# A hybrid attention and gating block in split fp32 on one core: first weights of two seven-product stages ahead of the bank reads, operand space opened to the plain stages, later splits for the next stage

## The chip, the cores and the metric

One NeuronCore of a Trainium2 chip runs the whole program; the host only lays the arrays out in the blocks that are loaded. The metric is the device time of one execution in microseconds, lower is better. The kernel before takes 2866.29 us (median of 3 runs, 2864.26 to 2869.96).

## The reference, cut to what matters

One decoder block on 512 tokens of width 2048, all in float32:

```
a = rms_norm(x);  z = a @ w_in          # q_lat 512, kv_lat 512, k_pe 64, u 1024, v 1024, gate logits 2 x 2048
y_attn = mla(q_lat, kv_lat, k_pe) @ w_o_attn          # 16 heads, causal, rotary part of 64
y_sgu  = (gelu(u) * (tril(w_s) v' + b_s)) @ w_o_sgu   # v' = rms_norm(gelu(v)), chunks of 128, 8 groups
h = x + (sigmoid(g0) * y_attn + sigmoid(g1) * y_sgu) @ w_out
f = rms_norm(h)
h = h + (silu(f @ w_gate) * (f @ w_up)) @ w_down      # hidden width 5632
return rms_norm(h)
```

## The kernel before, in words

**Split operands.** A float32 operand is kept as two float32r pieces, a rounded `hi` and the rest `lo`; ACT makes `hi` with a cast and DVE makes `lo` with a subtraction (`split` L134, `chunk` L150 to L157, `form_w` L367 to L372). Each product is three matmuls (`mm3` L168: lo by hi, hi by hi, hi by lo).

**Plain stages.** `gemm_fm` (L172) and `gemm_tm` (L185) take one weight block of 512 KB at a time. `chunk` loads it on the SP queue into a raw tile, makes `hi` and `lo`, and 24 matmuls with 512 columns follow. Plain stages are: the latents and the v half of the gating input (L277 to L352, 16 chunks of `w_v`), the attention pairs (L745 to L766), `sgu_out` (L732, 8 calls of two chunks), the attention output (L774 to L789), `w_out` (L820 to L847) and `w_down` (L900 to L909, 80 chunks).

**Seven-product stages.** `run` (L463) multiplies blocks with seven products in place of eight, each of 24 matmuls with 256 columns: once for u and both gates (L533, 20 blocks), once for the FFN's gate and up weights (L889, 44 blocks). `Unit.weights(i)` forms the i-th of seven weight combinations on DVE and splits it; `multiply` issues the matmuls, `read` empties the three banks. These are pinned to program order among themselves on each engine; everything else is placed by the scheduler of the framework. The moving operands are eight `forms` of 14 units each, made by `forms_x` (L320): four subtractions, one cast on ACT and one subtraction on DVE. Six of the eight forms are made while the plain stage in front still runs. `run` starts with weights 0 to 2, multiplies them by the six forms, calls `rest()` (L488; `x_rest` L528 or `f_rest` L850) for the last two forms, then loads `unit(1)` and goes on. At the end of its last block it calls the functions in `ends`, by the number of the product just issued.

**Reads of the stage in front.** For the first seven-product stage the eight banks of the v products are read before `run` is called (L357 to L362): per bank a Gelu, a Square that sums into `vacc` and a store to `vvd`. For the second, the loop at L820 to L847 adds x to each bank, squares, scales by `r0` and stores to `hd`, all before `run`. `rv` (L579 to L581) is the norm factor from `vacc`; `spatial` (L583) uses it in pairs 0 and 1 of the attention loop (L754).

**Space.** `Arena` hands out pieces of two big SBUF tiles, `ar` (144 units, operands) and `af` (52 units, float32), in program order. Its rule (L65 to L68) is the cost by which a free place is chosen:

```
cost = (i,) if low else (n < self.large and i < self.keep, n < 8 and self.pack and None not in block,
                         max(span), -i)
```

So a small piece goes to a place at or above `keep` if any is free there, however lately that place was given back (`max(span)` comes third), and only then to the place given back longest ago. `ar.keep` is NX = 112 through the whole kernel, `ar` has 144 units, and a chunk needs two pieces of 4. A piece that was used shortly before makes the new writer wait for the matmuls that still read it.

**Loads.** `load` and `store` go through the POOL queue, weights through SP. `latents(g)` (L264) loads four tiles, transposes on PE and splits; it is called after products 2 and 4 of the last block (L533). `hidden(k0, n)` (L886) loads and splits tiles of the FFN's hidden values, after products 2 and 4 of the last block (L889). The residual tiles `h` are loaded from `hd` right after (L892 to L894).

Of the kernel before, what the change touches and what calls it, by code (L numbers as in the profile page):

```python
# [12 lines left out]
AF = mybir.ActivationFunctionType  # L13
# [75 lines left out]
def tile_block(ctx: ExitStack, tc, a):  # L89
# [9 lines left out]
    def T():  # L99
        return af.get(2)  # L100
# [58 lines left out]
    def load(src):  # L159
        t = T()  # L160
        nc.gpsimd.dma_start(t, src)
        return t
# [101 lines left out]
    def latents(g):  # L264

        zs, rows = [load(latd[g, tb]) for tb in range(NB)], []
        for k in range(4):
            ps = PS()
            for tb in range(NB):
                nc.tensor.transpose(out=ps[:, tb * P:(tb + 1) * P], in_=zs[tb][:, k * P:(k + 1) * P], identity=ident)  # L270
            v = (V_Q, V_KV)[g] + k
            rows.append(split(ps, vec[:, v:v + 1]))
        drop(zs)
        return rows
# [82 lines left out]
    for tb in range(NB):  # L357
        for g in range(2):
            t = T()
            nc.scalar.activation(t, banks[g][tb], AF.Gelu_apprx_tanh, scale=rx[:, tb:tb + 1])  # L360
            nc.scalar.activation(junk, t, AF.Square, accum_out=vacc[:, tb * 2 + g:tb * 2 + g + 1])
            store(vvd[g, tb], t)  # L362
# [100 lines left out]
    def run(jobs, fx, rest, ends, lead=3):  # L463
# [12 lines left out]
        for g in range(last + 7 + lead + 1):  # L476
# [7 lines left out]
            if g == lead - 1:  # L484
                early = len(fx)
                for i in range(lead):
                    units[0].multiply(i, ready[i], fx, range(early))
                rest()  # L488
                unit(1)
# [9 lines left out]
        af.keep, af.pack = 0, False  # L499
# [28 lines left out]
    def x_rest():  # L528
        x_forms(6)
        x_forms(7)  # L530

    latT = []
    run(x_jobs(), fx, x_rest, {2: lambda: latT.append(latents(0)), 4: lambda: latT.append(latents(1))})  # L533
# [45 lines left out]
    vs2 = small(NB, "vs2")  # L579
    nc.vector.tensor_reduce(out=vs2, in_=vacc.rearrange("p (n k) -> p n k", k=2), axis=AX.X, op=ALU.add)  # L580
    rv = rsqrt(vs2, SGUW, NB, "rv")  # L581
# [163 lines left out]
    for pr in range(NP):  # L745
# [8 lines left out]
        if pr < 2:  # L754
            spatial(pr)
# [18 lines left out]

    oT = [move(load(ogd[k]), low=True) for k in range(KD)]
# [46 lines left out]
    for c in range(4):  # L822
# [13 lines left out]
        hs[c] = []  # L836
        for tb, ps in enumerate(banks):
            tt(ht[tb], ps, ht[tb], ALU.add)
            nc.scalar.activation(junk, ht[tb], AF.Square, accum_out=facc[:, c * NB + tb:c * NB + tb + 1])
            if c == 0 and tb == NB - 1:  # L840
                r0 = rsqrt(facc[:, :NB], D // 4, NB, "r0")
        for tb in range(NB):
            t = T()
            nc.scalar.activation(t, ht[tb], AF.Copy, scale=r0[:, tb:tb + 1])
            hs[c].append(t)
            store(hd[tb, :, c * 512:(c + 1) * 512], ht[tb])
# [4 lines left out]
    def f_rest():  # L851
        scaled(3)
        f_forms(6)
        f_forms(7)
        nc.vector.tensor_reduce(out=fs, in_=facc.rearrange("p (c n) -> p n c", c=4), axis=AX.X, op=ALU.add)
        rf = rsqrt(fs, D, NB, "rf")
        nc.vector.reciprocal(rest, r0)
        tt(rest, rest, rf, ALU.mult)
        row_bcast(rest, rxb)
# [25 lines left out]

    def hidden(k0, n):  # L886
        return [move(load(hidd[k])) for k in range(k0, k0 + n)]

    run(ffn_jobs(), ff, f_rest, {2: lambda: hid.extend(hidden(0, 4)), 4: lambda: hid.extend(hidden(4, 4))})  # L889


    for tb in range(NB):  # L892
        for c in range(4):
            h[tb][c] = load(hd[tb, :, c * 512:(c + 1) * 512])  # L894
# [5 lines left out]
    for k0 in range(0, 40, 8):  # L900
        nxt, n = [], 2 if k0 < 32 else 1
        for c in range(4):
            nxt += hidden(k0 + 8 + c * n, n)
# [127 lines left out]
```

## Time and profile before

| | |
|---|---|
| median of 3 runs | 2866.29 us (2864.26 to 2869.96) |
| the profiled execution | 2865.04 us; its span 2863.3 us |
| mean granted TensorE clock | 0.979 of full speed |
| busy, of the span | PE 2725.3 us (95%), DVE 1739.3 us (61%), ACT 1094.0 us (38%), POOL 197.3 us (7%) |
| read from HBM, written | 315.07 MB, 45.35 MB, 126 GB/s over the span |

The profile shows one execution. Matmuls overlap, so a PE that counts as busy may still run at half clock or with few matmuls; the number of matmuls in a stretch tells more. "Idle before" of an instruction is the time in which its engine had nothing to do, with the instruction that ended the wait. The 1.7 us between the span and the profiled execution's time lie outside the recorded instructions.

### The profile page before, as it was taken

The numbers are of one execution on the slowest core, as the hardware profiler recorded it, in microseconds if no ns is written. First come the engines' busy times: TensorE is split into PE (matmuls) and PEld (weight loads), VectorE is DVE, ScalarE is ACT, GpSimd is POOL, SyncE is SP. The second block draws the span as 40 slices with busy tenths as digits, with TensorE's granted clock in tenths as the row PEclk, the third lists the DMA queues.
The fourth block names the chain that finished last, engine by engine and source line by source line (L and its number), as shares of the span: only waits on it lengthen the run. The fifth ranks groups of instructions, "written<-read, shape, count | busy, mean of one in ns | idle before, by whom it ended". The sixth has DMA issues, their size and how long they took to land. (4 is left out here: it accounts for less than half of the span.)

```text
span 2863.3 us, 41568 instructions
## 1 busy us (share of the span) xinstructions
PE 2725.3 (95%) x17320; PEld 2479.6 (87%) x17320; DVE 1739.3 (61%) x2200; ACT 1094.0 (38%) x1534; POOL 197.3 (7%) x369
## 2 busy tenths in 40 slices
PE   8989999998999779999889999999999989999998
PEld 6879999987888558888789999999999978787786
DVE  5637777786666233333377877877878763443336
ACT  5334444454555122224344444444344441221224
POOL 1000000011002121000000000000000020000000
PEclk9999999999999889999989999999999989999999
DMA  7423333352324454434223333232333352442333
GB/s 293 157 98 111 140 118 140 118 170 89 103 74 148 132 183 148 129 114 140 88 99 130 115 115 133 104 126 104 133 108 125 114 200 89 146 140 67 103 110 118
DMA packets 103901, 363.13 MB, mean 127 GB/s; under 512 B 14177, under 2 KB 14177, under 8 KB 103713
## 3 DMA queue, kind: packets, MB, share of 16 engines
q1 hardware_dynamic: 72720, 260.60, 26.1%
q0 software_dynamic: 29552, 97.28, 10.1%
q8 instruction: 135, 2.21, 0.3%
q10 hardware_dynamic: 1440, 2.60, 0.3%
q14 instruction: 54, 0.43, 0.0%
HBM read 315.07 MB, written 45.35 MB: 126 GB/s over the span
## 5 line engine op out<-in xcount | busy, mean ns | idle before, releaser
L382 PE MATMUL b<-ar 128*128 128x256 f32 x3584 | 1021.9, 285 | 23.9 <-DVE ar L371 14.6
L384 PE MATMUL b<-ar 128*128 128x256 f32 x3584 | 1020.9, 285 | 3.4 <-DVE ar L119 3.4
L383 PE MATMUL b<-ar 128*128 128x256 f32 x3584 | 1020.3, 285 | 0.0
L169 PE MATMUL b<-ar 128*128 128x512 f32 (+1 forms) x2016 | 780.8, 388 | 95.9 <-DVE ar L155 51.0
L170 PE MATMUL b<-ar 128*128 128x512 f32 (+1 forms) x2016 | 773.8, 384 | 0.0
L171 PE MATMUL b<-ar 128*128 128x512 f32 (+1 forms) x2016 | 762.5, 383 | 0.1
L382 PEld LDWEIGHTS b<-ar 128*128 128x128 f32 x3584 | 694.5, 194 | 26.3 <-DVE ar L371 9.0
L384 PEld LDWEIGHTS b<-ar 128*128 128x128 f32 x3584 | 694.4, 194 | 4.1 <-DVE ar L119 4.1
L371 DVE TENSOR_TENSOR ar<-af,ar 128x1024 fp32r<-128x1024 f32 x448 | 544.3, 1223 | 248.8 <-ACT ar L370 247.4
L383 PEld LDWEIGHTS b<-ar 128*128 128x128 f32 x3584 | 694.5, 194 | 0.0
L370 ACT CAST ar<-af 128x1024 fp32r<-128x1024 f32 x448 | 459.3, 1046 | 481.6 <-DVE af L393 367.8
L169 PEld LDWEIGHTS b<-ar 128*128 128x128 f32 x2016 | 386.0, 191 | 186.7 <-ACT ar L154 48.5
L155 DVE TENSOR_TENSOR ar<-af,ar 128x1024 fp32r<-128x1024 f32 (+1 forms) x224 | 267.7, 1204 | 420.8 <-ACT ar L154 414.1
L154 ACT CAST ar<-af 128x1024 fp32r<-128x1024 f32 (+1 forms) x224 | 229.8, 1035 | 663.5 <-PE b L171 354.0
L171 PEld LDWEIGHTS b<-ar 128*128 128x128 f32 x2016 | 385.6, 191 | 75.8 <-DVE ar L155 2.4
L170 PEld LDWEIGHTS b<-ar 128*128 128x128 f32 x2016 | 386.2, 192 | 70.1
L393 DVE TENSOR_TENSOR af<-af 128x1024 f32<-128x1024 f32 x192 | 234.6, 1222 | 4.2
L390 DVE TENSOR_TENSOR af<-b,af 128x256 f32<-128x256 f32 x320 | 134.6, 421 | 20.3 <-PE b L384 17.4
L897 DVE SCALAR_TENSOR_TENSOR af<-b,rest,af 128x512 f32<-128x512 f32 x96 | 71.6, 749 | 118.1 <-PE b L171 118.1
L138 DVE TENSOR_TENSOR ar<-af,ar 128x512 fp32r<-128x512 f32 x100 | 66.4, 688 | 74.7 <-ACT ar L137 74.7
L396 ACT COPY af<-b 128x256 f32<-128x256 f32 x128 | 47.3, 370 | 166.0 <-PE b L384 131.8
L137 ACT CAST ar<-af 128x512 fp32r<-128x512 f32 x100 | 59.6, 619 | 133.1 <-DMA af<-hidd 46.0
(223 smaller groups left out, 1190.9 us busy)
## 6 DMA issues: line engine op xcount, KB each, us to landing
af<-in_w_gate SPq DMA_DIRECT2D x88, 512.0 KB, 5.3
af<-in_w_up SPq DMA_DIRECT2D x88, 512.0 KB, 5.4
af<-in_w_down SPq DMA_DIRECT2D x88, 512.0 KB, 4.2
af<-in_w_g SPq DMA_DIRECT2D x64, 512.0 KB, 5.3
af<-in_w_oattn SPq DMA_DIRECT2D x32, 512.0 KB, 3.5
af<-in_w_out SPq DMA_DIRECT2D x32, 512.0 KB, 3.5
hidd<-af POOLq DMA_DIRECT2D x44, 256.0 KB, 2.6
af<-hidd POOLq DMA_DIRECT2D x44, 256.0 KB, 3.3
```

The source lines that it names most:

```text
L154: nc.scalar.copy(hi[:, :n], raw[:, :n])
L155: nc.vector.tensor_tensor(out=lo[:, :n], in0=raw[:, :n], in1=hi[:, :n].bitcast(F32), op=ALU.subtract)
L169: nc.tensor.matmul(ps, sl, mh, start=first, stop=False)
L170: nc.tensor.matmul(ps, sh, mh, start=False, stop=False)
L171: nc.tensor.matmul(ps, sh, ml, start=False, stop=last)
L370: pin(nc.scalar.copy(hv, src))
L371: pin(nc.vector.tensor_tensor(out=lv, in0=src, in1=hv.bitcast(F32), op=ALU.subtract))
L382: pin(nc.tensor.matmul(ps, lo[:, ks], xh, start=first and kp == 0, stop=False, skip_group_check=True))
L383: pin(nc.tensor.matmul(ps, hi[:, ks], xh, start=False, stop=False, skip_group_check=True))
L384: pin(nc.tensor.matmul(ps, hi[:, ks], xl, start=False, stop=kp == 7, skip_group_check=True))
L390: pin(nc.vector.tensor_tensor(out=out, in0=in0, in1=in1, op=ALU.add))
L393: pin(nc.vector.tensor_tensor(out=out, in0=in0, in1=in1, op=ALU.subtract))
```

## The change

Four things change.

1. `run` calls `rest` in two parts: weights 0 to 2 of the first block come first, then the first part, then the products with the forms that exist, then the second part. For the first stage the first part is the reads of banks 0 to 3 and form 6, the second the reads of banks 4 to 7 and form 7; for the FFN the first part is the adding of x for the last column block, the second the transposes, forms 6 and 7, the squares, the stores and the norm. The Squares of v leave the reads; `v_stats` loads `vvd` again in pair 0 of the attention and squares there, and `spatial` moves to pairs 1 and 2.
2. `ar.keep` becomes 0 at the end of each `run` and NX again ahead of the attention output.
3. The tiles of the next stage: the loads of `latents` come after products 0 and 2, their transposes and splits after 4 and 5; four hidden tiles are loaded after product 1 and split after 4, the other four after 5.
4. The residual tiles `h` are loaded four at a time inside the first pass of `w_down`.

```diff
@@ latents
-    def latents(g):
-
-        zs, rows = [load(latd[g, tb]) for tb in range(NB)], []
+    def lat_in(g):
+        return [load(latd[g, tb]) for tb in range(NB)]
+
+    def latents(g, zs):
+
+        rows = []
@@ after the v products
-    for tb in range(NB):
-        for g in range(2):
+    def v_out(g):
+        for tb, ps in enumerate(banks[g]):
             t = T()
-            nc.scalar.activation(t, banks[g][tb], AF.Gelu_apprx_tanh, scale=rx[:, tb:tb + 1])
-            nc.scalar.activation(junk, t, AF.Square, accum_out=vacc[:, tb * 2 + g:tb * 2 + g + 1])
+            nc.scalar.activation(t, ps, AF.Gelu_apprx_tanh, scale=rx[:, tb:tb + 1])
             store(vvd[g, tb], t)
@@ run
             if g == lead - 1:
+                rest = rest()
+                next(rest)
                 early = len(fx)
                 for i in range(lead):
                     units[0].multiply(i, ready[i], fx, range(early))
-                rest()
+                for _ in rest:
+                    pass
                 unit(1)
...
-        af.keep, af.pack = 0, False
+        af.keep, af.pack, ar.keep = 0, False, 0
@@ first seven-product stage
     def x_rest():
+        v_out(0)
         x_forms(6)
+        yield
+        v_out(1)
         x_forms(7)
...
-    run(x_jobs(), fx, x_rest, {2: lambda: latT.append(latents(0)), 4: lambda: latT.append(latents(1))})
+    run(x_jobs(), fx, x_rest, {0: lambda: zs.append(lat_in(0)), 2: lambda: zs.append(lat_in(1)),
+                               4: lambda: latT.append(latents(0, zs[0])), 5: lambda: latT.append(latents(1, zs[1]))})
@@ attention
-    vs2 = small(NB, "vs2")
-    nc.vector.tensor_reduce(out=vs2, in_=vacc.rearrange("p (n k) -> p n k", k=2), axis=AX.X, op=ALU.add)
-    rv = rsqrt(vs2, SGUW, NB, "rv")
+    def v_stats():
+        for g in range(2):
+            for tb in range(NB):
+                t = load(vvd[g, tb])
+                nc.scalar.activation(junk, t, AF.Square, accum_out=vacc[:, tb * 2 + g:tb * 2 + g + 1])
+                drop(t)
+        vs2 = small(NB, "vs2")
+        nc.vector.tensor_reduce(out=vs2, in_=vacc.rearrange("p (n k) -> p n k", k=2), axis=AX.X, op=ALU.add)
+        return rsqrt(vs2, SGUW, NB, "rv")
...
-        if pr < 2:
-            spatial(pr)
+        if pr == 0:
+            rv = v_stats()
+        elif pr < 3:
+            spatial(pr - 1)
...
+    ar.keep = NX
     oT = [move(load(ogd[k]), low=True) for k in range(KD)]
@@ w_out, per column block c
+        def add_x(c=c, ht=ht, banks=banks):
+            hs[c] = []
+            for tb, ps in enumerate(banks):
+                tt(ht[tb], ps, ht[tb], ALU.add)
+                if c:
+                    t = T()
+                    nc.scalar.activation(t, ht[tb], AF.Copy, scale=r0[:, tb:tb + 1])
+                    hs[c].append(t)
...
+        elif c < 3:
+            add_x()
+            squares()
+            keep_h()
@@ FFN
     def f_rest():
+        add_x()
+        yield
         scaled(3)
         f_forms(6)
         f_forms(7)
+        squares()
+        keep_h()
...
+    def split_hidden():
+        hid[:4] = [move(t) for t in hid[:4]]
+
+    run(ffn_jobs(), ff, f_rest, {1: lambda: hid.extend(hidden_in(0, 4)), 4: split_hidden,
+                                 5: lambda: hid.extend(hidden(4, 4))})
...
-    for tb in range(NB):
-        for c in range(4):
-            h[tb][c] = load(hd[tb, :, c * 512:(c + 1) * 512])
@@ w_down
         for c in range(4):
+            for tb in range(NB if k0 == 0 else 0):
+                h[tb][c] = load(hd[tb, :, c * 512:(c + 1) * 512])
             nxt += hidden(k0 + 8 + c * n, n)
```

`squares` and `keep_h` are the old Square and store of the loop at L835 to L847, in functions of their own; for column block 0 the order of the old loop stays but for the stores, which come last.

## Rows read from the trace of the kernel before

**Rows 1.** Page, part 1: busy time and instructions of each engine.
```profile
PE 2725.3 (95%) x17320; PEld 2479.6 (87%) x17320; DVE 1739.3 (61%) x2200; ACT 1094.0 (38%) x1534; POOL 197.3 (7%) x369
```

**Rows 2.** Windows: stretch, length, busy us (instructions) of PE, PEld, DVE, ACT, POOL, clock, DMA, GB/s.
```profile
475.00:500.00 25.00, 25.00 (x210) 25.00 (x210) 18.78 (x20) 11.12 (x13) 1.08 (x2) 1.00 0.38 144
...
195.00:230.00 35.00, 20.67 (x104) 19.45 (x104) 24.43 (x35) 16.05 (x23) 2.17 (x4) 0.71 0.16 51
600.00:645.00 45.00, 39.12 (x264) 35.76 (x263) 38.96 (x56) 25.61 (x36) 11.56 (x21) 0.96 0.61 199
690.00:706.00 16.00, 10.48 (x48) 9.39 (x47) 8.58 (x24) 6.72 (x19) 3.84 (x7) 0.79 0.43 140
935.90:1063.00 127.10, 91.29 (x314) 69.37 (x312) 35.63 (x42) 25.24 (x32) 22.04 (x41) 0.85 0.45 139
1428.00:1460.00 32.00, 21.52 (x125) 19.63 (x124) 23.08 (x36) 15.71 (x22) 1.08 (x2) 0.73 0.24 87
2325.00:2350.00 25.00, 12.74 (x88) 12.34 (x86) 11.55 (x18) 8.05 (x14) 9.17 (x18) 0.77 0.62 201
2350.00:2375.00 25.00, 24.76 (x97) 19.84 (x98) 18.80 (x19) 15.78 (x19) 3.69 (x7) 0.89 0.94 347
2423.00:2800.00 377.00, 362.28 (x1568) 291.99 (x1567) 144.53 (x159) 84.81 (x95) 13.97 (x26) 1.00 0.34 110
```

**Rows 3.** Timeline of ACT, attention output stage: start, us, line, operation [idle before <-releaser].
```profile
1149.12 1.05 ACT L154 CAST ar<-af 128x1024 fp32r<-128x1024 f32 x1 [4.39 <-PE b L171]
...
1154.56 1.05 ACT L154 CAST ar<-af 128x1024 fp32r<-128x1024 f32 x1 [0.69 <-PE b L171]
```

**Rows 4.** Timeline of ACT in the calls of `sgu_out`, two chunks in a row.
```profile
936.31 1.04 ACT L154 CAST ar<-af 128x1024 fp32r<-128x1024 f32 x1 [8.48 <-PE b L171]
946.04 1.04 ACT L154 CAST ar<-af 128x1024 fp32r<-128x1024 f32 x1 [8.69 <-PE b L171]
```

**Rows 5.** Waits of PE, 900 to 1066 us: for whom, us in total, times, longest.
```profile
PE b L169 <- DVE ar L155: 38.4, 14, 4.5
```

**Rows 6.** All waits, 2385 to 2860 us: those of PE for chunks.
```profile
PE b L169 <- ACT ar L154: 14.5, 18, 1.4
```

**Rows 7.** Waits of PE, 590 to 930 us (attention).
```profile
PE b L169 <- DVE ar L155: 12.6, 8, 3.8
```

**Rows 8.** Groups by line: the Squares of v; busy us, mean ns, idle before.
```profile
L361 ACT ACTIVATE junk<-af 128x512 f32<-128x512 f32 x8 | 5.0, 626 | 0.1
```

**Rows 9.** DMA issues: tile, queue, count, KB each, median us to landing.
```profile
af<-in_w_ukv SPq DMA_DIRECT2D x16, 512.0 KB, 4.2
...
af<-vvd POOLq DMA_DIRECT2D x8, 256.0 KB, 4.2
```

**Rows 10.** Timeline of ACT in pair 0: the first Exp and its table.
```profile
652.65 1.28 ACT L699 ACT_TABLE_LOAD   x1
653.94 0.40 ACT L699 ACTIVATE af<-af,nm 128x128 f32<-128x128 f32 x1
```

**Rows 11.** Timelines of DVE and PE where the v products end and the first `run` starts.
```profile
198.50 0.16 DVE L580 TENSOR_REDUCE vs<-vacc 128x4 f32<-128x8 f32 x1 [22.45 <-ACT junk L361]
...
218.04 2.02 DVE L119 TENSOR_TENSOR ar<-af,ar 128x1792 fp32r<-128x1792 f32 x1 [1.75 <-ACT ar L330]
...
200.72 0.58 PE L382 MATMUL b<-ar 128*128 128x256 f32 x1 [5.50 <-DVE ar L371]
```

**Rows 12.** Timelines of DVE and PE where `w_out` ends and the FFN's `run` starts.
```profile
1448.06 3.96 DVE L119 TENSOR_TENSOR ar<-af,ar 128x1792 fp32r<-128x1792 f32 x2
...
1432.84 0.55 PE L382 MATMUL b<-ar 128*128 128x256 f32 x1 [4.50 <-DVE ar L371]
```

**Rows 13.** Timelines of ACT and PE where the FFN's `run` ends and `w_down` starts.
```profile
2330.22 1.22 ACT L137 CAST ar<-af 128x512 fp32r<-128x512 f32 x2 [4.13 <-DMA af<-hidd]
...
2334.03 0.58 PE L382 MATMUL b<-ar 128*128 128x256 f32 x1 [4.34 <-DVE af L390]
2350.20 0.80 PE L169 MATMUL b<-ar 128*128 128x512 f32 x1 [8.12 <-ACT ar L154]
```

More of the change, by code (lines that the diff above doesn't have):

```diff
@@ L528, in x_rest @@
     def x_rest():
+        v_out(0)
         x_forms(6)
+        yield
+        v_out(1)
         x_forms(7)
-    latT = []
-    run(x_jobs(), fx, x_rest, {2: lambda: latT.append(latents(0)), 4: lambda: latT.append(latents(1))})
+    latT, zs = [], []
+    run(x_jobs(), fx, x_rest, {0: lambda: zs.append(lat_in(0)), 2: lambda: zs.append(lat_in(1)),
+                               4: lambda: latT.append(latents(0, zs[0])), 5: lambda: latT.append(latents(1, zs[1]))})
     qnT, kvT = latT
@@ L835, in tile_block, with squares, keep_h @@
                 f_forms(order[c, kp])
[L836 to L841, printed above, removed]
-        for tb in range(NB):
[L843 to L846, printed above, removed]
+        def add_x(c=c, ht=ht, banks=banks):
[6 more added lines that the diff above has]
+                    hs[c].append(t)
+        def squares(c=c, ht=ht):
+            for tb in range(NB):
+                nc.scalar.activation(junk, ht[tb], AF.Square, accum_out=facc[:, c * NB + tb:c * NB + tb + 1])
+        def keep_h(c=c, ht=ht):
+            for tb in range(NB):
+                store(hd[tb, :, c * 512:(c + 1) * 512], ht[tb])
+        if c == 0:
+            add_x()
+            squares()
+            r0 = rsqrt(facc[:, :NB], D // 4, NB, "r0")
+            for tb in range(NB):
+                t = T()
+                nc.scalar.activation(t, ht[tb], AF.Copy, scale=r0[:, tb:tb + 1])
+                hs[0].append(t)
+            keep_h()
[3 more added lines that the diff above has]
+            keep_h()
     fs = small(NB, "fs")
@@ L851, in f_rest @@
     def f_rest():
+        add_x()
+        yield
         scaled(3)
@@ L854, in f_rest @@
         f_forms(7)
+        squares()
+        keep_h()
         nc.vector.tensor_reduce(out=fs, in_=facc.rearrange("p (c n) -> p n c", c=4), axis=AX.X, op=ALU.add)
@@ L884, in tile_block, with hidden_in @@
     hid, h = [], [[None] * 4 for _ in range(NB)]
+    def hidden_in(k0, n):
+        return [load(hidd[k]) for k in range(k0, k0 + n)]
     def hidden(k0, n):
-        return [move(load(hidd[k])) for k in range(k0, k0 + n)]
-    run(ffn_jobs(), ff, f_rest, {2: lambda: hid.extend(hidden(0, 4)), 4: lambda: hid.extend(hidden(4, 4))})
-    for tb in range(NB):
-        for c in range(4):
-            h[tb][c] = load(hd[tb, :, c * 512:(c + 1) * 512])
+        return [move(t) for t in hidden_in(k0, n)]
+    def split_hidden():
+        hid[:4] = [move(t) for t in hid[:4]]
+    run(ffn_jobs(), ff, f_rest, {1: lambda: hid.extend(hidden_in(0, 4)), 4: split_hidden,
+                                 5: lambda: hid.extend(hidden(4, 4))})
     def more(tb, c, ps):
```

## The prediction

> **What bounds the kernel now.** I read the page's busy times first: PE is busy 95% of the span and no other engine over 61% [rows 1], so time can only come back where PE stands or runs slowly. The windows show where. In a seven-product stage at full clock PE issues 210 matmuls in 25 us, 0.119 us each [rows 2]; in a plain stage one chunk of 24 matmuls takes 5.44 us, the distance of two casts that each wait for PE [rows 3], 0.2267 us each. Against these two rates six stretches lose time [rows 2]:
> - start of the first `run` (195 to 230 us): 104 matmuls are worth 12.4 us and take 35, 22.6 lost, clock 0.71;
> - end of that stage and first projections (600 to 645): PE idle 45 - 39.1 = 5.9;
> - `sgu_out` (935.9 to 1063): 314 matmuls are worth 71.2 us and take 127.1, **55.9 lost**, clock 0.85;
> - start of the FFN (1428 to 1460): 125 are worth at most 14.9 and take 32, 17 lost;
> - FFN to `w_down`: 88 x 0.119 = 10.5 of 25 us, then 97 x 0.2267 = 22 of 25, together 17.5 lost;
> - `w_down` (2423 to 2800): 1568 are worth 355.4 of 377, 21.6 lost.
>
> They are 140.5 us together. The reader should then ask what each wait ends on, stage by stage, since the share of 95% hides all of it.
>
> **The change, part by part.**
>
> *Operand space, `sgu_out`.* Casts start 9.7 us apart, each the moment a matmul ends [rows 4], and PE then waits 14 times for the subtraction, 38.4 us in all [rows 5]: cast, subtraction and 24 matmuls run one after the other. The cost line of `Arena.get` says why. 14 of the 16 pieces of `sgT` (two units each) lie at 112 and above; the one place of four left there, units 116 to 119, is taken by the first half of every chunk, because a place above `keep` beats an older one. With `keep` 0 the place given back longest ago wins; carried through the calls, a chunk's halves then lie on places given back many chunks earlier, so ACT and DVE can work ahead as in the attention output, where PE never waits. The cover is large: a chunk needs 1.04 us of ACT in 5.44 us of PE [rows 3, 4], and DVE is busy 35.63 of the 127.1 us [rows 2]. What is late next: the 16 tiles of `oT` take the lowest places, and seven or so of them are then places of `sgT` or of the last chunk, which come free only with the last matmuls; one split and its load stand open there. I leave 6 of the 55.9 us for that and for restarts of the clock. Gain 50, from 36 (half of the waits come back through `oT` and the POOL queue) to 54.
>
> *Operand space, `w_down`.* By the same rule 26 of the 80 chunks lie on a place given back one chunk before; PE waits 18 times for the cast, 14.5 us [rows 6], and the rest of the 21.6 is slow restarts. With `keep` 0 none does. Loads of `h` four at a time leave the same number of raw places (four). Gain 14, from 6 (ACT then waits for the loads) to 20.
>
> *Operand space, attention.* The first chunk of each projection is on a place just given back: 8 waits of PE, 12.6 us, the longest 3.8 [rows 7], which lies in the stretch from 600. Of the other 8.8 I count half, since DVE is busy then too. *Squares of v:* eight Squares of 0.63 us [rows 8] leave the path at the first `run` and come back in pair 0 behind eight loads on POOL of 4.2 us each [rows 9]. If ACT meets them landed they cost nothing, since PE waits mostly for others; if it waits for each in turn, 8 x 4.8 = 39 us. The nearest row is the stall in pair 1, where DVE waits for loads of `vvd` and PE loses 5.5 us between 690 and 706 us [rows 2]; that stall moves on with `spatial` to the next pair, and I add half of it again, 2.5. Net gain of the pairs 2, from -8 to 9.
>
> The root for `rv` also changes tables: it now lies between two Exps, so up to two table loads more. A load took 1.28 us and the next instruction started 0.01 us after its end [rows 10], so 2.6 us on ACT, inside the 2.5 above. The Trainium skill ("ScalarE: Activation LUTs", What ACT_TABLE_LOAD costs) adds a drain of about 1.38 us to each switch; by that my estimate would be 5.3 us and the forecast up to 2.8 us later. The trace shows no such drain behind this load, and I stay with the row.
>
> *First `run`.* DVE stands idle 22.45 us until the Squares end, and PE's first product waits 5.5 us for weights that were formed only after them [rows 11]. After: the raw weights are there, DVE is free, and the places of weights 0 to 2 are those of the chunks (6,0), (6,1) and (7,0), all free 5.4 us before the last matmul; so PE goes straight on. Three products with seven forms are 63 matmuls, 7.5 us. Form 7 is then the late one: reads of banks 4 to 7 end some 1.5 us after the last matmul, four stores and one load follow on POOL, then scaling, four subtractions, cast and subtraction; two forms kept DVE until 220 us before [rows 11]. I take form 7 as 12 us after the last matmul, 5 us of idle PE, 3 us of DVE behind, 2 us of low clock: 10 lost of 22.6. Gain 12.5, from 5 (the forms' chain is as late as before) to 17. In the queues: POOL gets four stores ahead of the load for form 6 and four more ahead of that for form 7; ACT has three casts ahead of the reads, and the third waits for a place until 5.4 us before the end, with the first reads behind it. That still ends before PE needs a bank.
>
> *End of that stage.* The loads of `latents` are issued earlier, the splits come later. The wait of 3.8 us [rows 7] goes; the splits after product 5 have 2.9 us until PE needs them. Gain 4, from 0 to 6.
>
> *FFN start.* PE waits 4.5 us for the first weights, and forms 6 and 7 end at 1452 us [rows 12]. After: weights 0 to 2 are ready when `w_out` ends; 54 matmuls, 6.4 us, cover the adding of x. Then the transposes, two forms (3.96 us for the last subtraction alone) and, behind them now, squares, norm and the broadcast of `rest`: 8.5 us stay lost. Gain 8.5, from 2 to 13.
>
> *FFN to `w_down`.* ACT stands on a hidden tile's load 4.13 us with the casts of the last weights behind it, PE then 4.3 us, and 8.1 us for the first chunk [rows 13], whose raw place was one of those the hidden tiles went through. After: four tiles load side by side before they are needed, splits come behind the last weights, and the first raw place is one of the block buffers that fell free long before. 5.5 stay of 17.5. Gain 12, from 5 to 16.
>
> *Sum:* 50 + 14 + 2 + 12.5 + 4 + 8.5 + 12 = **103 us**. Against the profiled execution (2865.0, span 2863.3 plus 1.7) that is 2762; the median of the runs lies 1.3 higher, so 2763.
>
> **Rivals.**
> - *The starts give it back.* Late forms 6 and 7 and their chain bound both starts as before: 5 + 2 in place of 21, and `w_down` 6 in place of 14: gain 81, 2785. For it: DVE is the engine that PE waits for there.
> - *`sgu_out` is held by something else.* If `oT`, loads of `g1d` behind stores on POOL or a low clock keep half its loss, gain 25 less: 2788. Against it: the same shape in the attention output has the same queues and no waits [rows 3]. If the least-recently-freed rule still met fresh places, this is the case where the change does not do what it says.
> - *More comes back*, each part near its upper end: 2735.
> - *Slower: casts run ahead of the softmax.* With free places everywhere the scheduler may put the 32 chunk casts of the eight pairs ahead of Exp on ACT, each standing until its load lands. ACT serves in order, as the stall at 2330 shows [rows 13]. At 4.2 us a landing [rows 9] that is up to 134 us, 2866 - 103 + 134 = 2897. It turns the sign only where a cast waits over 103 / 32 = 3.2 us on average, close to a whole landing; against it, raw tiles are loaded well ahead.
>
> **How the numbers follow.** Forecast (gains of 85 to 120) 0.62; starts 0.12; `sgu_out` 0.12; more 0.10; slower 0.04. The likeliest is 2763. The range leaves out the slower case and the ends: 2738 to 2803, the lower end with `w_down` and the starts near their best, the upper with two of the small-gain cases partly together. The measurement tells 0.2%, 6 us, from no change; all cases but the last are faster by more: faster 0.95, same 0.01, slower 0.04.
>
> **What would show it.** In the new trace: `sgu_out` takes about 80 us at clock 1.00, casts there no longer end on PE; PE's waits for casts in `w_down` fall under 5 us; after the last v product PE goes on at once and then stands some 5 us for form 7; at the FFN start the first wait is for form 6 or 7, not for weights; the 8 us wait ahead of the first `w_down` chunk is gone; in pair 0 ACT waits for `vvd`. I am wrong if `sgu_out` still needs over 105 us, or if ACT in the pairs waits for weight loads.

## The result, and the profile after

The kernel after takes 2733.94 us (median of 4 runs, 2731.53 to 2738.27) where the kernel before, run beside it, takes 2865.28 (2863.24 to 2869.96): a ratio of 0.954, with an interval of 0.952 to 0.956. It is faster by 131 us; 103 were forecast. The direction was right; the measured time lies 4 us below the lower end of the range. The profiled execution took 2731.94 us, 133.1 less than the one before.

Page, part 1, of the kernel after (busy us, share of the span, instructions):
```profile
PE 2679.5 (98%) x17320; PEld 2458.8 (90%) x17320; DVE 1731.3 (63%) x2200; ACT 1093.6 (40%) x1534; POOL 201.4 (7%) x377
```
Against [rows 1] PE has the same instructions and 46 us less busy time, because before many of them took longer: in `sgu_out` 95.36 / 332 = 0.287 us each at a granted clock of 0.86, after it 76.39 / 339 = 0.225 at 1.00. So the share says little; time by stage says more. Both traces were cut at the same seven points of the work: end of the v products, first projection, last store to `ogd`, last store to `ysd`, end of `w_out`, first product of `w_down`, last product. Windows (columns as in [rows 2]), the kernel before, cut at these points:
```profile
195.22:627.00 431.78, 415.42 (x3393) 413.98 (x3394) 328.38 (x367) 201.64 (x249) 28.84 (x53) 0.98 0.35 127
627.00:931.83 304.83, 284.06 (x1678) 252.30 (x1677) 201.46 (x391) 162.68 (x348) 37.55 (x69) 0.98 0.35 111
931.83:1064.11 132.28, 95.36 (x332) 72.73 (x330) 36.74 (x44) 26.00 (x32) 23.13 (x44) 0.86 0.46 144
1064.11:1428.35 364.24, 358.17 (x1584) 295.98 (x1584) 139.50 (x164) 110.97 (x141) 28.87 (x54) 0.99 0.40 128
1428.35:2350.20 921.85, 898.92 (x7416) 896.91 (x7416) 724.49 (x827) 380.61 (x465) 38.99 (x74) 0.98 0.33 120
2350.20:2854.05 503.85, 489.09 (x2112) 395.82 (x2112) 210.62 (x264) 125.42 (x169) 19.61 (x37) 0.99 0.35 116
```
The same windows of the kernel after:
```profile
195.21:615.37 420.16, 411.56 (x3393) 410.41 (x3393) 312.59 (x349) 192.47 (x234) 28.39 (x53) 0.99 0.36 130
615.37:907.88 292.51, 280.47 (x1678) 251.50 (x1677) 207.45 (x407) 176.41 (x374) 41.71 (x77) 0.98 0.39 127
907.88:984.27 76.39, 76.39 (x339) 63.25 (x338) 31.33 (x40) 20.06 (x27) 23.11 (x44) 1.00 0.66 226
984.27:1343.35 359.08, 354.77 (x1581) 293.40 (x1580) 145.58 (x170) 111.92 (x139) 28.00 (x53) 1.00 0.39 131
1343.35:2241.97 898.62, 893.22 (x7418) 891.80 (x7417) 713.77 (x814) 378.24 (x464) 33.63 (x63) 1.00 0.33 122
2241.97:2720.64 478.67, 478.67 (x2112) 396.15 (x2110) 214.10 (x271) 128.24 (x173) 25.76 (x48) 1.00 0.39 127
```
Read the first number after each pair of times, the length, one list against the other:

| stretch | before | after | gain | forecast |
|---|---|---|---|---|
| first start and its stage | 431.8 | 420.2 | 11.6 | 12.5 |
| eight pairs | 304.8 | 292.5 | 12.3 | 2, and 4 for the end of the stage in front |
| `sgu_out` | 132.3 | 76.4 | 55.9 | 50 |
| attention output, `w_out` | 364.2 | 359.1 | 5.2 | 0 |
| FFN, with the way into `w_down` | 921.9 | 898.6 | 23.2 | 8.5 + 12 |
| `w_down` and the last blocks | 503.9 | 478.7 | 25.2 | 14 |

The gains sum to 133.4, the forecasts to 103. In `sgu_out` and from 2242 us on PE is busy for the whole window. In [rows 4] ACT's casts in `sgu_out` waited for PE; now they wait for loads, and the first cast for the attention output comes 54.6 us ahead of the last store to `ysd` (984.27). ACT's timeline after, between 905 and 990 us:
```profile
927.28 1.05 ACT L154 CAST ar<-af 128x1024 fp32r<-128x1024 f32 x1 [3.94 <-DMA af<-in_w_osgu]
929.62 1.05 ACT L154 CAST ar<-af 128x1024 fp32r<-128x1024 f32 x1 [1.29 <-DMA af<-in_w_oattn]
```
The stretches that answer to [rows 2], in windows of the kernel after:
```profile
195.00:230.00 35.00, 26.40 (x181) 25.25 (x181) 23.39 (x29) 12.95 (x14) 1.68 (x4) 0.85 0.27 94
1343.00:1375.00 32.00, 27.29 (x204) 26.07 (x203) 24.05 (x40) 18.31 (x28) 1.85 (x4) 0.89 0.46 165
2225.00:2250.00 25.00, 25.00 (x178) 23.58 (x178) 17.14 (x24) 14.68 (x21) 8.40 (x16) 1.00 0.69 225
2300.00:2677.00 377.00, 377.00 (x1665) 312.26 (x1664) 151.72 (x174) 87.53 (x103) 15.05 (x28) 1.00 0.35 112
```
Both starts still lose time: 181 x 0.119 = 21.5 us of work in 35, and 204 x 0.119 = 24.3 in 32. In `w_down` 377 us now hold 1665 matmuls, 1568 before. What PE still waits for, over the whole run (the six largest rows of its waits: us in total, times, longest):
```profile
PE b L169 <- ACT ar L154: 11.6, 2, 10.8
PE b L169 <- DVE nm L712: 9.5, 2, 7.7
PE b L386 <- DVE ar L119: 5.4, 4, 1.6
PE b L169 <- DVE ar L155: 4.2, 2, 3.2
PE b L384 <- ACT ar L333: 3.4, 2, 1.8
PE b L384 <- DVE af L392: 3.2, 3, 2.0
```
The 10.8 us lie at the head of the program and are in both kernels. The 7.7 stand in pair 1, where 5.5 stood before [rows 2]; the 3.2 at the head of the attention output. Of the first, second and fourth row 0.8 us more lie in `w_out` and 2.7 in the pairs; the other three rows belong to the two starts, but for 0.7 us.

### The profile page after: what moved, and what is told of

The parts are those of the page before. It is cut to its first block, busy times and chain, and to the rows that moved or that the text cites. A ratio compares the mean times of both kernels' runs of the same rounds, so it can differ in the third digit from the quotient of the medians.

```text
span 2729.9 us, 41675 instructions
## 1 busy us (share of the span) xinstructions
PE 2679.5 (98%) x17320; PEld 2458.8 (90%) x17320; DVE 1731.3 (63%) x2200; ACT 1093.6 (40%) x1534; POOL 201.4 (7%) x377
## 4 chain that ended last, share of the span: by engine, by line
PE 82%; issue 9%; DMA 4%; DVE 3%; ACT 1%; POOL 1%; SPq 0%; POOLq 0%; ACTq 0%; DVEq 0%
PE b L384 15%; PE b L386 15%; PE b L385 15%; PE b L169 12%; PE b L171 12%; PE b L170 12%; DMA af<-in_xT 1%; DVE ar L373 1%; DMA af<-in_w_uq 1%; ACT ar L372 1%; DVE af L395 0%; PE b L732 0%; DVE af L392 0%; DMA sgd<-af 0%; DMA af<-in_w_lat 0%
## 5 line engine op out<-in xcount | busy, mean ns | idle before, releaser
L169 PE MATMUL b<-ar 128*128 128x512 f32 (+1 forms) x2016 | 766.3, 380 | 25.3 <-ACT ar L154 11.6
L171 PE MATMUL b<-ar 128*128 128x512 f32 (+1 forms) x2016 | 763.8, 379 | 0.3 <-DVE ar L155 0.3
L170 PE MATMUL b<-ar 128*128 128x512 f32 (+1 forms) x2016 | 764.0, 379 | 0.0
```

Of the source, the lines that this page charges most:

```text
L169: nc.tensor.matmul(ps, sl, mh, start=first, stop=False)
L170: nc.tensor.matmul(ps, sh, mh, start=False, stop=False)
L171: nc.tensor.matmul(ps, sh, ml, start=False, stop=last)
```

## The experiments

**Operand space alone, and all but it.** The first is the kernel before with two lines of the change, the second the kernel after without them.
```diff
-        af.keep, af.pack = 0, False
+        af.keep, af.pack, ar.keep = 0, False, 0
...
+    ar.keep = NX
     oT = [move(load(ogd[k]), low=True) for k in range(KD)]
```


> The kernel before with the operand space alone: keep becomes 0 at the end of each seven-product stage and 112 again ahead of the attention output; nothing else of the change. Places theory (what the plain stages lost was the wait for a place given back one chunk earlier, and the restart of PE behind each such wait): sgu_out from the last attention store to the last ysd store falls from 132.3 us to 76 to 78, w_down with its tail from 503.9 to 479 to 481 although h is still loaded in one go, the eight pairs give 8 to 10 us, both starts and the stretch between the FFN and w_down stay as they were; 2773 to 2782 us in all. Rival (the loads of h in fours and the later splits gave half of w_down's and the pairs' part): w_down 490 or more, the pairs 4 us or less, 2790 or more.

> The kernel after without the operand space: keep stays 112 through the whole kernel, all the rest of the change stays. Places theory: sgu_out is back at 130 to 134 us, w_down with its tail at 498 to 504 although h is loaded in fours, the pairs lose 8 to 10 us, attention output and w_out stay at 359; 2818 to 2830 us in all. Rival (loads of h in fours): w_down stays at 490 or less and the whole at 2812 or less. Second rival (the five microseconds that w_out gained come from the places that the earlier stages left behind): attention output and w_out go back to 364.

Measured: 2768.3 us for the space alone (before beside it: 2866.7), 2831.9 without it. Windows of the space alone: pairs, `sgu_out`, attention output with `w_out`, FFN, `w_down`:
```profile
627.27:916.69 289.42, 281.71 (x1683) 252.68 (x1682) 205.76 (x396) 167.90 (x353) 40.00 (x73) 0.99 0.36 123
916.69:995.90 79.21, 79.21 (x351) 65.63 (x350) 33.28 (x42) 20.11 (x27) 21.55 (x40) 1.00 0.68 235
995.90:1351.90 356.00, 351.50 (x1562) 290.57 (x1560) 136.07 (x160) 109.81 (x140) 28.96 (x55) 0.99 0.37 128
1351.90:2276.13 924.23, 900.76 (x7416) 898.75 (x7416) 724.36 (x827) 380.70 (x465) 38.94 (x74) 0.98 0.33 120
2276.13:2757.02 480.89, 480.84 (x2112) 397.35 (x2112) 211.76 (x264) 127.03 (x169) 19.86 (x37) 1.00 0.36 122
```
Windows of all but the space: pairs, `sgu_out`, `w_down`:
```profile
620.90:935.75 314.85, 286.61 (x1678) 254.09 (x1679) 201.05 (x397) 169.72 (x364) 40.60 (x74) 0.97 0.34 113
935.75:1064.29 128.54, 94.87 (x332) 72.19 (x330) 37.10 (x45) 26.34 (x32) 24.80 (x46) 0.87 0.45 145
2321.91:2820.57 498.66, 485.39 (x2112) 394.04 (x2110) 214.15 (x273) 127.96 (x174) 25.86 (x48) 1.00 0.36 122
```
In `sgu_out` the space alone leaves nothing to lose: 351 matmuls in 79.21 us are 0.2257 each (its last store comes a few products of the next stage later, hence 351 and not 339). It takes 23.0 us from `w_down`, with all of `h` loaded in one go, and 15.4 from the pairs, where 8 to 10 were expected; the start is as before, the FFN 2.4 us longer, and the whole 5 us under its range. Without the space `sgu_out` and `w_down` are slow again, and the pairs are 10.0 us *slower* than in the kernel before. That is 22.3 more than in the kernel after, where 8 to 10 were expected, and the whole is 2 us above its range. PE's wait of 3.8 us, 12 us into the first projections [rows 7], is still there without the space. PE's timeline of that kernel:
```profile
633.19 0.77 PE L169 MATMUL b<-ar 128*128 128x512 f32 x1 [3.86 <-DVE ar L155]
```
With the space alone PE waits for no chunk in the pairs. Over the six stretches the space alone gives 98.2 us (2658.8 to 2560.6) and the rest 34.1 (to 2624.8), together 132.2 of the 133.4. So the two halves add up over the whole. Stretch by stretch they do not: the pairs would gain 15.4 - 10.0 = 5.4 and gained 12.3; `sgu_out` with the attention output and `w_out` would gain 61.3 + 9.0 = 70.3 and gained 61.1. The rival, that loads of `h` or later splits carry `w_down`, falls: all but the space gives 5.2 us there. The second rival falls for the operand places: attention output and `w_out` take 359.0 us without the space. The places of the float32 tiles, which stay as in the kernel after in that run, are another matter (see "What no term held").

**More places under the old rule.** The kernel before, with
```diff
-        af.keep, af.pack = 0, False
+        af.keep, af.pack, ar.keep = 0, False, 96
...
+    ar.keep = NX
     oT = [move(load(ogd[k]), low=True) for k in range(KD)]
```


> The kernel before with keep 96 in place of 112 in the plain stages behind each seven-product stage: half as many places again for the chunks, but the rule that a place above keep is taken however lately it was given back stays. By the kernel's own order of gets and puts all 32 pieces of sgu_out and 117 of 160 in w_down then lie on a place given back one or two chunks before (14 and 70 in the kernel before). Places theory (age counts, not number): no gain anywhere; sgu_out 125 to 150 us, w_down 500 to 520, 2855 to 2900 us in all. Rival (number of places counts): sgu_out near 105, w_down near 492, the whole at 2825 or less.

Measured: 2844.8 us, 21.9 under the kernel before. Neither theory had it whole. Windows of `sgu_out` and `w_down`, then two casts in a row from ACT's timeline in `sgu_out`:
```profile
925.85:1035.75 109.90, 85.90 (x334) 65.83 (x332) 37.65 (x45) 26.25 (x32) 23.61 (x44) 0.94 0.55 185
2324.26:2833.38 509.12, 491.37 (x2112) 395.59 (x2112) 211.32 (x264) 125.88 (x169) 19.88 (x37) 0.99 0.34 114
```
```profile
961.59 1.05 ACT L154 CAST ar<-af 128x1024 fp32r<-128x1024 f32 x1 [2.60 <-PE b L169]
968.65 1.05 ACT L154 CAST ar<-af 128x1024 fp32r<-128x1024 f32 x1 [6.01 <-PE b L169]
```
`w_down` became slower by 5.3 us with half as many places again, as age would have it and number would not; the stage differs by up to 2.7 us (478.7 to 481.4) between the kernels here that give its chunks old places. `sgu_out` improved all the same: by the kernel's own order of gets and puts, 14 of the 16 chunks now have their first half (the cast's) on a place given back *two* chunks before, and all have the second half (the subtraction's) on one given back one chunk before. The cast runs ahead, only the subtraction still stands behind the last matmul, and the distance of two casts falls from 9.7 us [rows 4] to 7.1 in the two shown, and from 9.8 to 7.9 on the average of thirteen casts in a row. So age decides, and it decides for each half by itself.

**The order at the end of `w_out`'s blocks.** The kernel after, with the squares between the additions and each copy followed by its store for blocks 0 to 2, as before:
```diff
-        if c == 0:
-            add_x()
...
-        elif c < 3:
-            add_x()
-            squares()
-            keep_h()
+        if c < 3:
+            hs[c] = []
+            for tb, ps in enumerate(banks):
+                tt(ht[tb], ps, ht[tb], ALU.add)
+                nc.scalar.activation(junk, ht[tb], AF.Square, accum_out=facc[:, c * NB + tb:c * NB + tb + 1])
...
```


> The kernel after with the old order at the end of each of the first three column blocks of w_out (squares between the additions, each scaled copy followed by its store of h); the last block and all else as in the kernel after. Order theory (the stall of 4.6 us at the end of w_out is gone because the copies no longer stand behind all squares and stores): attention output and w_out go from 359.1 back to 363 to 365, 2738 to 2740 us. Rival (the stall went with something else of the change): 359 and 2732 to 2736.

Measured: 2741.4 us; 361.3 for attention output and `w_out`, between the two. Yet the wait near the end of `w_out` is 0.8 us as in the kernel after, and what is longer is PE's wait at the *head* of the attention output, 5.0 for 3.2. The pairs too were 4.4 us longer, with work that the edit does not touch, and the whole lies above both ranges. The order theory falls. The kernels below that leave this order and `oT` alone have 359.7 to 368.2 us here.

**The Squares back in their place.** The kernel after, with two edits at once, the Squares and the pairs of `spatial`:
```diff
             nc.scalar.activation(t, ps, AF.Gelu_apprx_tanh, scale=rx[:, tb:tb + 1])
+            nc.scalar.activation(junk, t, AF.Square, accum_out=vacc[:, tb * 2 + g:tb * 2 + g + 1])
             store(vvd[g, tb], t)
...
-        if pr == 0:
-            rv = v_stats()
-        elif pr < 3:
-            spatial(pr - 1)
+        if pr in (0, 2):
+            spatial(pr // 2)
```


> The kernel after with the Squares of v back beside the Gelus that empty the banks (no second load of vvd, rv ready before the pairs) and spatial in pairs 0 and 2. Theory (the move of the Squares costs more in the pairs than it gives at the start, since form 7 waits for its load and not for ACT): from the last v product to the first projection 420 to 422 us as now, the eight pairs 284 to 289 in place of 292.5; 2724 to 2731 us in all. Rival (the start needs the Squares out of the way, as the prediction argued): 424 to 426 at the start, pairs 288 or more; 2732 to 2738.

Measured: 2734.3 us. The start is 422.4 (2.2 longer), the pairs 285.5 (7.0 shorter), much as the theory says; the total is above its range because attention output and `w_out` took 365.4, with two waits of 3.1 and 4.5 us. Window of the pairs:
```profile
617.59:903.11 285.52, 277.86 (x1678) 249.07 (x1677) 206.98 (x401) 169.87 (x356) 38.11 (x71) 1.00 0.37 125
```
All four profiles with the Squares back (this one, the two edits together below, and the kernel with the ring twice) have 285.5 to 288.8 us in the pairs; the kernel after and the four others that keep its pairs have 292.2 to 296.9. So in start and pairs the move of the Squares, with `spatial` behind it, costs more than it gives. How much of the 7.0 is the Squares and how much the free pair between the two halves of `spatial` stays open.

**Form 7's load.** The kernel after, with
```diff
     def x_rest():
+        raws = [x_load(6), x_load(7)]
         v_out(0)
-        x_forms(6)
+        x_forms(6, raws[0])
         yield
         v_out(1)
-        x_forms(7)
+        x_forms(7, raws[1])
```
where `x_load` is the first line and the load of `x_forms`. Timelines of POOL and PE in the kernel after, the load of form 7 and the matmul that its second half releases:
```profile
201.35 0.54 POOL L341 DMA_DIRECT2D af<-in_xT  x1 [4.00 <-DVE ar L119]
...
211.83 0.39 PE L386 MATMUL b<-ar 128*128 128x256 f32 x1 [1.55 <-DVE ar L119]
```


> The kernel after with the raw tiles of forms 6 and 7 taken and loaded at the head of the first part, before the banks are read; nothing else. Theory (form 7 is late because its load stands in the POOL queue until the last subtraction of form 6 frees its place, and DVE then waits 4.0 us for it): PE's second pair of waits for a form at 209.8 and 211.8 comes 4 to 8 us earlier, from the last v product to the first projection 413 to 417 us in place of 420.2; 2726 to 2731 us. Rival (the reads of the banks and the two forms on DVE set the time themselves): 418.5 or more, 2731 to 2737.

Measured: 2731.5 us; the start with its stage is 416.4, 3.8 shorter. The matmul that answers, from PE's timeline of this kernel:
```profile
208.12 0.39 PE L390 MATMUL b<-ar 128*128 128x256 f32 x1 [1.04 <-DVE ar L119]
```
It comes 3.7 us earlier, and 4.4 earlier counted from the last v product (16.6 us behind it in the kernel after, 12.2 here), at the low end of the 4 to 8 expected. So the load was what form 7 waited for.

**The way into `w_down`.** Twice the kernel after: once with the hidden tiles loaded and split after products 2 and 4 as before, once with the loads of `h` in one go behind the FFN.
```diff
-    run(ffn_jobs(), ff, f_rest, {1: lambda: hid.extend(hidden_in(0, 4)), 4: split_hidden,
-                                 5: lambda: hid.extend(hidden(4, 4))})
+    run(ffn_jobs(), ff, f_rest, {2: lambda: hid.extend(hidden(0, 4)), 4: lambda: hid.extend(hidden(4, 4))})
```
```diff
+    for tb in range(NB):
+        for c in range(4):
+            h[tb][c] = load(hd[tb, :, c * 512:(c + 1) * 512])
...
-            for tb in range(NB if k0 == 0 else 0):
-                h[tb][c] = load(hd[tb, :, c * 512:(c + 1) * 512])
```


> The kernel after with the tiles of w_down loaded and split as before, four after product 2 and four after product 4 of the last block. Theory (the split that stands on its load in front of the last weights' casts is what cost time there): the FFN's stage grows by 3 to 5 us and PE stands 6 to 9 us before the first product of w_down; from the end of w_out to the first product of w_down 908 to 912 us in place of 898.6; 2743 to 2749 us in all. Rival (the sixteen loads of h ahead of the weights' and hidden tiles' loads cost it): 900 or less and 2732 to 2738.

> The kernel after with all sixteen loads of h in one go behind the FFN, as before. Theory (h is needed late and its loads wait for nobody): first product of w_down right behind the FFN's last, w_down with its tail 478.7 to 480; 2731 to 2738 us. Rival (the loads of h take the raw places and the POOL queue from the hidden tiles of the next pass): waits of PE on casts come back, w_down 484 or more, 2739 or more.

Measured: 2736.7 and 2745.3 us. Windows of the FFN with the way into `w_down`, old split times first, then old loads of `h`:
```profile
1348.17:2246.78 898.61, 893.19 (x7418) 891.78 (x7418) 714.92 (x816) 378.19 (x464) 34.20 (x64) 1.00 0.34 122
1343.71:2253.38 909.67, 893.06 (x7417) 891.48 (x7416) 716.78 (x821) 379.55 (x466) 39.64 (x74) 0.99 0.34 123
```
Both theories fell, and the rivals had the cause: with the old split times the FFN and the way into `w_down` take 898.6 us, the same as after; with the old loads of `h` 909.7, PE standing 11.1 us before the first product of `w_down` (the waits inside `w_down` that the second rival expected did not come: 480.9 us). The kernel with old loads, SP's waits and then SP's timeline (first issue of a `w_down` block), between 2215 and 2270 us:
```profile
SPq L153 <- DMA af<-hidd: 48.8, 1, 48.8
```
```profile
2246.01 24.01 SPq L153 DMA_DIRECT2D af<-in_w_down  x12
```
The kernel after, the same timeline between 2215 and 2265 us:
```profile
2230.76 33.82 SPq L153 DMA_DIRECT2D af<-in_w_down  x11
```
Sixteen tiles of `h` hold 32 of the 52 float32 units, so the raw tile of the first weight block shares what is left with the hidden tiles and its load stands behind one of them: 2246.0 in place of 2230.8. Once it is issued early, the split times do not matter.

**A version that beats both.** First the two edits that had shortened the start and the pairs, together; then also a ring for the tiles of `oT`. SP's waits of the kernel after, 930 to 1010 us, say why:
```profile
SPq L153 <- DVE ar L138: 46.2, 4, 40.1
```
A weight load of the attention output stands 40 us behind a split of `oT`, whose tile has its place, while PE soon waits for a block. By the kernel's order of gets and puts, weight blocks 3 to 7 of the attention output take places that tiles of `oT` gave back; with the ring they take places of earlier weight blocks.
```diff
-    oT = [move(load(ogd[k]), low=True) for k in range(KD)]
+    ring, oT = [T() for _ in range(4)], []
+    for k in range(KD):
+        nc.gpsimd.dma_start(ring[k % 4], ogd[k])
+        oT.append(split(ring[k % 4], low=True))
+    drop(ring)
```


> The kernel after with two edits together: the raw tiles of forms 6 and 7 loaded at the head of the first part, and the Squares of v back beside their Gelus with spatial in pairs 0 and 2. If the two gains are independent, as the theory has it (one is the wait for a load, the other DVE and ACT work in the pairs), the start with its stage is 416 to 419 us (416.4 with the early loads alone, 422.4 with the Squares alone) and the pairs are 284 to 287; with 359 to 366 for attention output and w_out 2720 to 2729 us in all. Rival (with the loads early, ACT is what form 7 waits for, and the Squares stand in front of its cast): 420 or more at the start, 2727 or more in all.

> The same two edits, and the sixteen tiles of oT loaded through a ring of four float32 tiles in place of one place each. Theory (the wait of 3 to 7 us at the head of the attention output comes from the SP queue: the raw tile of its third or fourth weight block lies on a place that a tile of oT still holds, so that the load stands for 40 us behind a split): no wait of PE over 1.5 us between 980 and 1010 us, attention output and w_out 355 to 360; 2716 to 2726 us in all. Rival (oT's splits wait for the operands of the last products of sgu_out, and the ring, with only four loads under way, makes them later): the wait is 5 us or longer, 2726 us or more.

Measured: 2734.8 and 2722.2 us. Together the first two give 417.6 at the start and 287.1 in the pairs, as expected; the total missed its range, since attention output and `w_out` took 368.2. With the ring that stretch is 350.8. Windows of this kernel, `sgu_out` and attention output with `w_out`:
```profile
902.12:981.51 79.39, 79.39 (x352) 65.75 (x351) 30.07 (x37) 17.60 (x22) 21.00 (x40) 1.00 0.65 225
981.51:1332.30 350.79, 349.88 (x1568) 289.75 (x1567) 146.57 (x173) 113.54 (x142) 29.71 (x56) 1.00 0.38 131
```
The two stretches are 430.2 us together, 435.5 in the kernel after: no wait is left at the border, and under a microsecond in the rest. SP still stands 37.5 us there, now for a store to `ysd`, but PE waits for nothing behind it. The ring also shifts the float32 places of `w_out`: the wait of 4.6 us there, which the kernel with the first two edits has, is 0.6. Then the kernel after and the one with the three edits were timed side by side.

> The kernel after itself, timed again beside the kernel with the ring. Theory (its own runs differ by several microseconds because the wait at the head of the attention output, 3 to 7 us in the kernels seen, and the stalls of spatial in pairs 1 and 2 depend on when loads land): median 2731 to 2738 us, single runs 5 us or more apart. Rival (every run is alike and the kernels differ by their edits alone): runs within 2 us of each other.

> The kernel with early loads for forms 6 and 7, the Squares beside the Gelus, spatial in pairs 0 and 2 and the ring of four tiles for oT, timed. Theory (each of the three edits takes away a wait that the kernel after has in every run): median 2718 to 2726 us, its interval below that of the kernel after, and its runs closer together than those of the kernel after, since the wait at the attention output is gone. Rival (the one run seen was a lucky landing of loads): median 2728 us or more, intervals that overlap.

Measured: the kernel after 2735.87 us (2734.51 to 2737.83), 0.956 of the kernel before (0.9544 to 0.9575); with the three edits 2719.71 (2717.98 to 2724.20), 0.9504 (0.9488 to 0.952). The intervals do not meet: 16 us more are to be had. That its runs would lie closer together was wrong: they span 6.2 us, those of the kernel after 3.3, where 5 or more were expected.

## Why the prediction was wrong in size

**The terms of the operand space were too small.** The prediction gave them 50 + 14 + 4.4 (half of the pairs' waits) = 68; the space alone gave 98.2. All the other terms (first start 12.5, end of its stage 4, Squares -2.5, FFN 8.5, way into `w_down` 12) came to 34.5; all but the space gave 34.1. So nearly the whole miss is one step, taken three times: finding the right waits and then leaving a part of them standing without a row that kept it. The table shows it by stretch: of the 30.4 us by which the forecast fell short, `w_down` has 11.2, the pairs with the end of the stage in front 6.3, `sgu_out` 5.9; `w_out` has 5.2 and the FFN 2.7, and the start gave 0.9 less than forecast.
- `w_down`, "Gain 14" of 21.6: 23.0 from the space alone. The 14 is about what the waits alone come to [rows 6]; the rest, which the prediction calls slow restarts, it left standing. PE was idle 14.7 us there [rows 2]; the other 6.9 were matmuls slower than the steady rate, and they went with the waits. The row also covers only 377 of the stage's 504 us: over all of it 503.85 - 2112 x 0.2267 = 25.1 us were lost.
- `sgu_out`, "I leave 6 of the 55.9": nothing stayed. The mechanism, a half that is written to a place just given back (the first half of each chunk), is what the traces and the kernel with 96 show. The border to the attention output, where the 6 were meant to fall, did get a wait, of 3.2 us, but behind this stretch.
- Pairs, "I count half, since DVE is busy then too": DVE was busy 201 of 305 us there. The eight waits of [rows 7] are one of 0.9 us after. The longest of them, 3.8, the prediction gave to the end of the stage in front and its later splits; the run without the space still has it, so it was the space's too. What the earlier loads of `latents` took away there is PE's wait of 2.0 us for their tiles.

**The rest was right in sum, by luck, and not in its terms.** Form 7 was ready 16.6 us after the last v product (195.2 to 211.8), not 12, and 12.2 with its load early; the start lost 13.5 us, not 10. The load in POOL's queue, named in the prediction, was priced too low, as the early load shows. The FFN's start lost 32 - 24.3 = 7.7, forecast 8.5. The way into `w_down` lost nothing where 5.5 were left, and of the two causes named the raw place was the one: the loads of `h` in fours are worth 11 us, the late splits nothing. The Squares were named with the right stall and too small a price: "2.5" for the pairs; all but the space has them 10.0 us slower (PE waits 10.2 us for the softmax there, 6.6 before, and 4.0 behind the root), and the Squares back, with `spatial` spaced out, 7.0 faster. ACT met the eight tiles of `vvd` landed, so the bound of 39 us was far off; the stall is `spatial`'s tiles on the raw places of the weights. In pair 0 two more table loads came, the root's and the one behind it, but both kernels have 12 in all: before, the root's stood at 199.42 us and the one behind it at 238.16, so the prediction charged the move and left out what it saved. ACT's timeline after:
```profile
645.56 1.28 ACT L201 ACT_TABLE_LOAD   x1
646.86 0.21 ACT L201 ACTIVATE rvr<-rvv 128x4 f32<-128x4 f32 x1
```
The next instruction starts 0.02 us behind the load's end (0.01 in [rows 10]). The Trainium skill ("ScalarE: Activation LUTs", What ACT_TABLE_LOAD costs) has a drain of about 1.38 us with each switch; this row does not show it behind the load.

**What no term held.** The stall in `w_out` (the wait of 4.6 us on one weight block) was left out of the sum; 5.2 us came back there. The order at the blocks' ends is not its cause. PE's waits for a cast in `w_out`: the kernel before, the kernel after, the kernel after with the Squares back:
```profile
PE b L169 <- ACT ar L154: 4.6, 1, 4.6
PE b L169 <- ACT ar L154: 0.8, 1, 0.8
PE b L169 <- ACT ar L154: 4.5, 1, 4.5
```
The wait is 4.4 to 4.6 us in the kernel before, with the space alone, with keep 96, with the Squares back and with the first two edits together; it is 1.0 or less in all others. By the order of gets and puts, the raw tile of the 28th of the 32 blocks, the one that PE waits for, takes in exactly those five kernels a place that `scaled` gave back one block before, and in the others a place given back three blocks before. So this wait went with the move of the Squares and of `spatial`, whose tiles shift the float32 places behind them; nothing in the prediction aimed at it. Part of the gain is lost again in the wait at the head of the attention output: 2.7 to 7.1 us in the kernels with the rest of the change, none with the ring. Why it is 3.2 us in one profile of the kernel after and 6.4 in another stays open.

**The rivals.** The case that came was the third, "each part near its upper end", 2735 us. It had a chance of 0.10, and the range began at 2738, above its own figure. `sgu_out` was held by nothing else. The slower case has its sign, but not its price: ACT stands 17.1 us on loads of the projections' weights in the pairs, 8.4 before, and PE pays for one of these waits, not for 32. In pair 1 ACT stands on the load of a chunk, and the subtraction of that chunk on DVE stands in front of the softmax that PE then waits 7.7 us for. ACT's timeline after, and SP's waits between 693 and 706 us:
```profile
708.67 1.78 ACT L154 CAST ar<-af 128x768 fp32r<-128x768 f32 x2 [9.42 <-DMA af<-in_w_uq]
```
```profile
SPq L153 <- DMA sgd<-af: 7.8, 1, 7.8
```
The load is late because its raw place was a tile of `spatial` on its way to `sgd`, so this is the same stall as above; nowhere else in the pairs does PE wait over 2 us.

## What to carry to other kernels

When a wait is traced to a place given back too lately, and the engines that make the operand have time to spare, count all of its time: the idle rows, and the slow matmuls behind them. Leave a part standing only for a row that names what holds it next. In an allocator look at how long ago a place was given back, for each piece of an operand by itself; and when many tiles are loaded early, ask whose weight loads will stand behind their places, since that is where the pairs, `oT`, `w_out` and `h` all lost time.

## What the runs showed that was not expected

- Idle time is not the whole price of a short wait: in `w_down` before, 14.7 us of idle stood for 21.6 lost, and in `sgu_out` before, 132.28 - 95.36 = 36.9 for 57 (332 x 0.2267 = 75.3 in 132.28), there at a granted clock of 0.86. With the waits gone both run at 1.00.
- The same order of work differs from run to run. A second profile of the kernel after took 5.9 us longer than the first (2737.83 for 2731.94), with the wait at the head of the attention output at 6.4 us in place of 3.2. Its pairs took 292.5 us in the first profile, and 296.9 in the kernel that differs from it only in `w_out`. A single look at a kernel is good to some 5 us; the windows of a stage tell more than the total. PE's waits of the second profile:
```profile
PE b L169 <- DVE ar L155: 7.2, 2, 6.4
```
